# A one-core hybrid encoder layer: maxima and sums change tilings through DRAM, weights' factors queue behind turned weights' parts, the norm's weights come as one row, and the first gates' steps are reordered

## The chip, the cores and the metric

The kernel runs on one core of a Trainium2 chip. The core has five engines that run side by side, each with its own queue of instructions that it takes in order: TensorE (PE in the profile; its weight loads are PEld), VectorE (DVE), ScalarE (ACT), GpSimd (POOL) and SyncE (SP), which here issues nearly all DMAs. Data moves between DRAM and the on-chip memory by DMA; matmuls write into eight PSUM banks.

The metric is the device time of one execution in microseconds (us), as the median of several runs. The profile is one such execution with every instruction recorded.

## What is computed

One layer over 1024 positions of width 1024. The input is normalised and projected to nine parts; branch A is a gMLP with mixing inside chunks of 128 positions, branch B an attention of 8 heads over three dilated windows; both are gated, projected, summed, projected again, normalised and added to the input.

```python
h    = rms_norm(x, g_pre)
u_a, v_a, z_a, q_b, k_b, v_b, z_b, gate_a, gate_b = split(h @ w_in)
y_a  = spatial_gating(gelu(u_a), gelu(v_a), ln_g, ln_b, w_s, b_s) * silu(z_a)
y_b  = mixture_of_dilations(q, k, v) * silu(z_b)     # patterns (128,1), (512,4), (2048,16)
g_a, g_b = sigmoid(gate_a + b_gate[:1024]), sigmoid(gate_b + b_gate[1024:])
x    = x + rms_norm((g_a * (y_a @ w_pa) + g_b * (y_b @ w_pb)) @ w_o, g_post)
# mixture_of_dilations: one windowed softmax per pattern (scores minus ALiBi slope * distance),
# the outputs weighted by the softmax over the three log-denominators
```

## The kernel before

All products are made in float32 accuracy from parts: an operand is split into a high part (ScalarE copies it, L106 or L159) and a low part (VectorE or GpSimd subtracts, L108 or L160), and a product is three matmuls: high by high, high by low, low by high.

The program is written in an order, but it isn't the order in which the engines run it. A planner gives every engine its list ahead of time: at each moment of its own simulated clock it takes the instruction that is ready there, earlier written ones first. On the chip each engine then keeps to its list. Where the chip is slower than planned, an engine stands at the head of its list though later entries could run.

**Start (L202 to L342, pool `sp`).** The norm's weights `gpre` are loaded as 128 copies of one row (L218). 14 matmuls on an empty tile warm TensorE up (L223). `norm_tile` (L232) squares one tile of x on ScalarE (L240), makes the factor (L241, L164, L165), applies it and `gpre` on VectorE (L245), transposes the result on TensorE (L229) and splits it into `hT`. Around the first two tiles stand the loads and splits of the weights of the first product (`row_pair`, L315), and, one for each pair of rows, `spatial_weights` (L280): it turns four groups of the mixing weights (L290), splits them and stores them to `ws_d`, sums their rows (`wsR`, L297), and forms their bias (`wsB`, L302) for `wsb_d`. The values of branch B (`vb`) follow in five groups of products (L322); between their steps (`ahead`) the other tiles of x are normalised and summed. The last stores of `vb` (L258) go from tiles of the pool `sp`.

**Projections (L351 to L577, pool `ap`).** The other projections save one product in eight: `seven` (L373) makes seven half-size products from sums of the quarters of weights (`s1` to `s4`) and of the inputs (`r11`, `r21`, `r22`, `t1` to `t4`), in the order of `STEPS` (L348): p1, p6, p2, p7, p5, p4, p3. p2 goes on in p1's bank, p4 in p7's and p3 in p5's; so p1 must first be copied out of its bank (L388, tile `u2`). The first call is `gates(0)` (L483). Its working tiles lie where the pool `sp` was, so they wait until that pool's last users are done.

**Attention (L580 to L930).** A head's scores come in two tilings: `half` 1 has queries by residue and 512 keys, `half` 0 has chunks. For each of 8 blocks of a tiling VectorE subtracts the bias and takes the maximum (L667), and ScalarE makes the exponentials and their sum (L671); maximum and sum lie in `own`. `exchange` brings them into the other tiling: 16 small copies of 32 partitions for each half, on GpSimd for half 0 and on VectorE for half 1 (L684). `normalise` (L688) joins the two tilings' maxima and sums into one factor for each query and block (`nm`). `scale` (L705) applies it to the weights: `half` 1 on VectorE (L710), most of `half` 0 on ScalarE (L712), two blocks on GpSimd (L708). `weigh` (L718) then turns the weights on TensorE (`keys`, L730; the tiles are named `pb`, `pa` and `pe`), splits the turned weights into `pth` and `ptl` (L733), and multiplies them by the values (L749, L764). The turned weights alternate between two banks; a bank is free once `ptl` is made from it.

The main loop (L902) runs nine stages for each head: the stages of `weigh` for head h, the scores of head h+1 beside them, the queries and keys of head h+2, and as filler the steps of branch A's last product (`mlp_products`, L849; the tiles `pa`, L872 to L874, with its weights `wr_pa`, `wl_pa`). In stage 3 stand the value loads of the next head and `exchange` for half 0, in stages 6 and 7 `exchange` for half 1, in stage 8 `normalise` and the first factors, then the loads `va` and `ve` (L621, L622). Inside `weigh` the factors of stage i+2 follow the turned weights of stage i (L801).

Of the kernel before, what the change touches and what calls it, by code (L numbers as in the profile page):

```python
# [18 lines left out]
P = 128  # L19
# [17 lines left out]
def tile_hybrid_encoder(  # L37
# [120 lines left out]
    def split(hi, lo, src, low=nc.vector):  # L158
        nc.scalar.activation(hi, src, AF.Copy)  # L159
        low.tensor_tensor(lo, src, f32(hi), ALU.subtract)  # L160
# [29 lines left out]
    wo_d = hi_lo("wo", [2, KT, P, 512])  # L190
    wsb_d = dram.tile([4, P, 4, P], F32, name="wsb_d")
# [10 lines left out]
    with tc.tile_pool(name="start", bufs=1) as sp:  # L202
# [15 lines left out]
        nc.scalar.dma_start(gpre, g_pre.to_broadcast([P, D]))  # L218
# [3 lines left out]
        for _ in range(14):  # L222
            nc.tensor.matmul(pt, idle[:, :P], idle, start=True, stop=True)  # L223

        def transposed(hl, i, src, name):

            pt = bank("pv", name)
            for k in range(4):
                nc.tensor.transpose(pt[:, k * P:(k + 1) * P], src[:, k * P:(k + 1) * P], ident)  # L229
            split(*[t[:, :, i * P:(i + 1) * P] for t in hl], pt.rearrange("p (k n) -> p k n", k=4))  # L230

        def norm_tile(c, load=1):  # L232
# [6 lines left out]
            for j in range(2):  # L239
                nc.scalar.activation(sq, xt[:, 512 * j:512 * (j + 1)], AF.Square, accum_out=ss[:, j:j + 1])  # L240
            nc.vector.tensor_tensor(ss[:, 0:1], ss[:, 0:1], ss[:, 1:2], ALU.add)  # L241
            power(ss[:, 1:2], ss[:, 0:1], 1.0 / D)
            for j in range(2):
# [3 lines left out]
                transposed(hT[j][b], i, xs, f"xT{c}{j}")  # L247
# [59 lines left out]
        norm_tile(0, 0)  # L307
        rows = sp.tile([32, P], F32, name="rows")
        nc.scalar.dma_start(rows[0:16, :], b_gate.rearrange("o (k p) -> (o k) p", p=P))
        nc.scalar.dma_start(rows[16:32, :], ln_g.rearrange("o (k p) -> (o k) p", p=P))  # L310
# [40 lines left out]
    with tc.tile_pool(name="proj", bufs=1) as ap:  # L351
# [21 lines left out]
        def seven(name, units, product_of, use):  # L373
# [3 lines left out]
            acc, u2, u3 = {}, {}, {}  # L377
            for n, weights, rn in STEPS:
                into = {"p2": "p1", "p4": "p7", "p3": "p5"}.get(n)
                if into:  # L380
                    pss = acc[into]
                else:
                    pss = acc[n] = [bank(t, f"{name}{n}{u}") for u, t in enumerate(units[n].split())]
                product_of(n, weights, R[rn], pss, into is None)
                for u, ps in enumerate(pss):
# [12 lines left out]
                    if n in ("p5", "p4", "p3"):  # L398
                        use(*{"p5": (1, 1), "p4": (1, 0), "p3": (0, 1)}[n], u, c, c)
                yield  # L400

        def features(w, c0, name, use, pool=ap):
# [16 lines left out]
            return seven(name, {"p1": "mm", "p6": "tp", "p7": "sc", "p5": "sc"}, product_of, use)  # L419
# [63 lines left out]
        take(gates(0, pool=None))  # L483
# [96 lines left out]
    with tc.tile_pool(name="heads", bufs=1) as hp, tc.tile_pool(name="attn", bufs=1) as ap:  # L580
# [45 lines left out]
        def scores(h, res):  # L626
# [4 lines left out]
            own = res["own"] = hp.tile([P, 2, 8, 2], F32, tag="own", bufs=2, name=f"own{h}")  # L631
            wts = res["wts"] = {}
            order = [(1, (i, i + 1)) for i in (0, 2, 4, 6)] + [(0, (1, 2)), (0, (3, 4)), (0, (5, 6)), (0, (0, 7))]
            for half, pair in order:
# [31 lines left out]
                for t, idx in enumerate(pair):  # L666
                    nc.vector.tensor_tensor_reduce(st[:, t, :n], ps[:, t, :n], biases[t], -1.0, -NEG, ALU.add, ALU.min,  # L667
                                                   own[:, half, idx, 0:1])
                for t, idx in enumerate(pair):
                    wts[half, idx] = st[:, t, :n]  # L670
                    nc.scalar.activation(st[:, t, :n], st[:, t, :n], AF.Exp, bias=own[:, half, idx, 0:1], scale=-1.0,  # L671
                                         accum_out=own[:, half, idx, 1:2])
                yield

        def exchange(h, res, half):

            own = res["own"]
            if half == 0:
                res["oth"] = ap.tile([P, 2, 8, 2], F32, tag="oth", bufs=2, name=f"oth{h}")
            for i in range(4):  # L680
                for j in range(4):
                    src = own[32 * i:32 * (i + 1), 1 - half].rearrange("p (b a) s -> p b a s", a=4)[:, :, j, :]
                    dst = res["oth"][32 * j:32 * (j + 1), half].rearrange("p (b a) s -> p b a s", a=4)[:, :, i, :]
                    (nc.gpsimd, nc.vector)[half].tensor_copy(dst, src)  # L684
                if i % 2:
                    yield

        def normalise(h, res):  # L688
# [3 lines left out]
            dd = ap.tile([P, 2, 2, 8], F32, tag="dd", bufs=2, name=f"dd{h}")  # L692
            nm = ap.tile([P, 2, 8], F32, tag="nm", bufs=2, name=f"nm{h}")
            nc.vector.tensor_tensor(nm, own[:, :, :, 0], oth[:, :, :, 0], ALU.min)
            nc.vector.tensor_tensor(dd[:, 0], nm, own[:, :, :, 0], ALU.subtract)
            nc.vector.tensor_tensor(dd[:, 1], nm, oth[:, :, :, 0], ALU.subtract)
            nc.scalar.activation(dd, dd, AF.Exp)
            nc.vector.tensor_tensor(nm, dd[:, 0], own[:, :, :, 1], ALU.mult)
            nc.vector.tensor_tensor(dd[:, 1], dd[:, 1], oth[:, :, :, 1], ALU.mult)
# [4 lines left out]

        def scale(res, half, idx):  # L705
            w, f = res["wts"][half, idx], res["nm"][:, half, idx:idx + 1]
# [11 lines left out]
        def weigh(h, res):  # L718
# [6 lines left out]
            def keys(jobs, n, w, name):  # L725
# [7 lines left out]
                split(hi[:n, :w], lo[:n, :w], pt[:n, :w])  # L733
# [168 lines left out]
        for h in range(H):  # L902
# [4 lines left out]
            for i in range(9):  # L907
# [173 lines left out]
```

## Time and profile before

| | us |
|---|---|
| median of 3 runs | 1569.66 |
| lowest and highest run | 1565.85, 1571.71 |
| the profiled execution | 1570.04 |
| its span (first to last instruction) | 1568.3 |

Busy time by stretch of the span, in us:

| stretch | what runs | TensorE | VectorE | ScalarE | GpSimd |
|---|---|---|---|---|---|
| 0 to 134 | norm, values of B | 124.97 | 61.49 | 56.35 | 39.65 |
| 134 to 152 | first gates | 15.06 | 7.11 | 5.73 | 6.98 |
| 152 to 980 | projections, mixing | 823.52 | 500.07 | 342.12 | 460.02 |
| 980 to 1340 | heads, beside them branch A's last product | 327.82 | 241.97 | 234.40 | 188.02 |
| 1340 to 1568 | last products | 218.32 | 52.93 | 47.16 | 87.58 |

How to read the lines below. A line of the timeline has the start, the duration, the engine, the line of the kernel, the operation, output<-input, shapes and the count; in brackets stands the time that the engine sat idle before it and what it waited for last. SPq and ACTq are the queues that issue DMAs; a duration there is that of issuing, not of the transfer. A line of waits has who waited for whom, the total in us, how often, and the longest. The tables by stretch have the busy time and count of instructions for each engine, then the clock that TensorE was granted (1.00 is full speed), the busy share of the DMA engines, and GB/s.

### The profile page before, as it was taken

The page shows a single profiled execution, that of the slowest core. Times are in us where ns is not written, and L with a number is a line of the kernel's source. Part 1 is how long each engine was busy: PE and PEld are TensorE (multiplying, and loading weights), DVE is VectorE, ACT ScalarE, POOL GpSimd, SP SyncE. Part 2 cuts the span into 40 slices and gives each one's busy share as a digit, 9 for nine tenths or more (in the row PEclk, how much of TensorE's full clock was granted, in tenths as well). Part 3 has the DMA queues.
Part 4 walks back from the last instruction along what each step waited for, and adds up shares of the span by engine and source line. Part 5 has one row for each costly group of instructions (what it writes and reads, how often), then busy time and mean ns, then how long its engine had stood idle before and what let it go on. Part 6 is the DMA issues. An engine that isn't in the chain of part 4 may idle for free.

```text
span 1568.3 us, 22757 instructions
## 1 busy us (share of the span) xinstructions
PE 1509.7 (96%) x7863; PEld 1276.0 (81%) x7863; DVE 863.6 (55%) x1698; ACT 685.8 (44%) x1315; POOL 782.3 (50%) x711
## 2 busy tenths in 40 slices
PE   8999999999999999999999999989998889999998
PEld 4787999988888888788888888867887778878886
DVE  5722544476665675756665564577666767232112
ACT  5522433343433433343445454577666756331111
POOL 3412644465655555565555555446544554473132
PEclk9999999999999999999999999999998999999999
DMA  8455433344534452535434343497686766885531
GB/s 264 155 173 178 128 106 102 113 128 131 170 119 145 136 166 95 163 126 163 140 123 132 119 150 118 147 267 229 198 217 175 221 212 180 249 263 166 190 108 67
DMA packets 247940, 252.16 MB, mean 161 GB/s; under 512 B 14312, under 2 KB 187400, under 8 KB 247568
## 3 DMA queue, kind: packets, MB, share of 16 engines
q1 hardware_dynamic: 247456, 249.88, 51.0%
q8 instruction: 62, 1.02, 0.3%
q10 hardware_dynamic: 368, 0.82, 0.1%
q14 instruction: 54, 0.44, 0.1%
HBM read 174.10 MB, written 76.55 MB: 160 GB/s over the span
## 4 chain that ended last, share of the span: by engine, by line
PE 72%; DVE 8%; ACT 5%; issue 5%; DMA 4%; POOL 3%; SPq 1%; DVEq 0%; ACTq 0%; POOLq 0%
PE pb L996 2%; PE pb L995 2%; PE pb L997 2%; PE pa L872 2%; PE pa L873 2%; PE pa L874 2%; PE sg L527 2%; PE vb L154 1%; PE vb L156 1%; PE vb L155 1%; POOL out L1016 1%; ACT st L671 1%; DVE oth L684 1%; DMA vn<-v_d 1%; PE pr L749 1%
## 5 line engine op out<-in xcount | busy, mean ns | idle before, releaser
L108 POOL TENSOR_TENSOR wl_pa<-wr_pa,wh_pa 128x512 fp32r<-128x512 f32 x56 | 74.8, 1345 | 46.8 <-ACT wh_pa L106 44.2
L516 DVE TENSOR_SCALAR vn<-vn,mean,rstd 128x128 f32<-128x128 f32 x128 | 58.6, 512 | 35.2 <-DMA vn<-v_d 34.8
L671 ACT ACTIVATE st<-st,own 128x256 f32<-128x256 f32 (+1 forms) x128 | 62.7, 492 | 34.9 <-DVE own L667 34.6
L995 PE MATMUL pb<-yh,wh_pb 128*128 128x512 f32 x128 | 50.6, 395 | 1.7 <-ACT yh L159 1.7
L996 PE MATMUL pb<-yl,wh_pb 128*128 128x512 f32 x128 | 50.8, 396 | 0.5 <-DVE yl L160 0.3
L106 ACT ACTIVATE wh_pa<-wr_pa 128x512 fp32r<-128x512 f32 x64 | 38.7, 625 | 28.1 <-PE pa L873 13.2
L997 PE MATMUL pb<-yh,wl_pb 128*128 128x512 f32 x128 | 50.3, 393 | 0.0
L684 DVE COPY oth<-own 32x4 f32<-32x4 f32 x128 | 35.7, 279 | 14.1 <-ACT st L671 12.6
L1030 ACT ACTIVATE sq<-o 128x512 f32<-128x512 f32 x16 | 9.6, 598 | 74.7 <-PE o L1028 74.7
L730 PE MATMUL pb<-ident,st 128*128 128x128 f32 x128 | 21.6, 292 | 21.0 <-DVE ptla L160 15.6
L160 POOL TENSOR_TENSOR vl<-vn,vh 128x512 fp32r<-128x512 f32 x32 | 41.3, 1291 | 0.8 <-ACT vh L159 0.8
L999 POOL TENSOR_TENSOR mb<-thb,mb 128x512 f32<-128x512 f32 x16 | 20.6, 1286 | 41.7 <-DVE thb L998 32.2
L160 POOL TENSOR_TENSOR qcl<-q,qch 128x512 fp32r<-128x512 f32 x16 | 27.6, 1732 | 26.0 <-ACT qch L159 25.5
L817 POOL TENSOR_TENSOR o<-o,zt 128x512 f32<-128x512 f32 x16 | 20.6, 1292 | 36.3 <-DMA zt<-z_d 20.0
L1010 DVE TENSOR_TENSOR sso<-sso 128x1 f32<-128x1 f32 x8 | 1.3, 160 | 67.6 <-ACT sq L1030 67.6
L730 PEld LDWEIGHTS pb<-ident,st 128*128 128x128 f32 x128 | 16.2, 148 | 26.9 <-DVE ptla L160 17.7
L684 POOL COPY oth<-own 32x4 f32<-32x4 f32 x128 | 24.0, 187 | 23.8 <-ACT st L671 18.8
L667 DVE CUSTOM_DVE_ANT_0 st<-sc,tb 128x256 f32<-128x256 f32 x64 | 23.7, 420 | 21.0 <-PE sc L664 19.7
L165 POOL TENSOR_TENSOR sso<-sso,mhalf 128x1 f32<-128x1 f32 x8 | 4.4, 550 | 59.1 <-DVE sso L164 59.1
L160 DVE TENSOR_TENSOR ptlb<-pb,pthb 128x512 fp32r<-128x512 f32 x32 | 21.9, 687 | 20.5 <-ACT pthb L159 20.3
L108 POOL TENSOR_TENSOR wl_wos<-wr_wos,wh_wos 128x512 fp32r<-128x512 f32 x16 | 20.7, 1291 | 22.8 <-ACT wh_wos L106 22.8
L108 POOL TENSOR_TENSOR wl_vb<-wr_vb,wh_vb 128x512 fp32r<-128x512 f32 x14 | 18.8, 1352 | 23.8 <-ACT wh_vb L106 23.8
(2643 smaller groups left out, 5852.9 us busy)
## 6 DMA issues: line engine op xcount, KB each, us to landing
wr_pa<-in_w_proj_a_dram SPq DMA_DIRECT2D x32, 512.0 KB, 5.5
wr_g<-in_w_in_dram SPq DMA_DIRECT2D x16, 512.0 KB, 3.5
wr_va<-in_w_in_dram SPq DMA_DIRECT2D x16, 512.0 KB, 3.8
wr_u<-in_w_in_dram SPq DMA_DIRECT2D x16, 512.0 KB, 4.1
wr_z<-in_w_in_dram SPq DMA_DIRECT2D x16, 512.0 KB, 3.7
vn<-v_d SPq DMA_DIRECT2D x32, 256.0 KB, 2.7
y_d<-s SPq DMA_DIRECT2D x32, 256.0 KB, 3.1
wr_yf<-y_d SPq DMA_DIRECT2D x16, 512.0 KB, 6.2
```

Source lines behind the costliest of these rows:

```text
L106: nc.scalar.activation(hi, src, AF.Copy)
L108: low.tensor_tensor(lo, src, f32(hi), ALU.subtract)
L160: low.tensor_tensor(lo, src, f32(hi), ALU.subtract)
L516: nc.vector.tensor_scalar(vn[:, c, :], vn[:, c, :], mean[:, 4 * b + c, 0:1], rstd[:, 4 * b + c:4 * b + c + 1], op0=ALU.subtract, op1=ALU.mult)
L527: nc.tensor.matmul(pg[:, 256 * c:256 * (c + 1)], w[:, 2 * cp + c, :], wst, start=(w is vh and c == 0), stop=(w is vl and c == 1), skip_gro ...
L671: nc.scalar.activation(st[:, t, :n], st[:, t, :n], AF.Exp, bias=own[:, half, idx, 0:1], scale=-1.0, accum_out=own[:, half, idx, 1:2])
L684: (nc.gpsimd, nc.vector)[half].tensor_copy(dst, src)
L730: nc.tensor.transpose(pt[:n, c0:c0 + P], src, ident)
L872: nc.tensor.matmul(pss[m], lh[:, k, :], rh, start=(q == 0 and k == 0), stop=False)
L995: nc.tensor.matmul(ps, lh, rh, start=(k == 0), stop=False)
L996: nc.tensor.matmul(ps, lh, rl, start=False, stop=False)
L997: nc.tensor.matmul(ps, ll, rh, start=False, stop=(k == KT - 1))
```

## The change

1. **Norm's weights as one row.** `g_pre` is loaded into one partition; two matmuls with a row of ones spread it over 128 partitions, and ScalarE copies the result. The warm-up is 4 matmuls before and 8 behind these. A one-column square is put first on ScalarE.
2. **Order at the start.** The splits of the first weights on ScalarE are queued behind the first tile's squares; the loads of `b_gate` and `ln_g` too. The four `spatial_weights` move from between the weight loads into the steps of the first product, behind the first tile's transposes on TensorE and its squares on ScalarE.
3. **First gates.** `gates(0)` runs p1, p6, p5, p2, p7, p4, p3; the use of p5 waits in its bank until p7 has been used.
4. **Maxima and sums through DRAM.** `exchange` stores `own` of one tiling to DRAM and loads it back with four loads of 32 partitions, all on SP; the layouts of `own`, `oth`, `dd` and `nm` change with it.
5. **Factors behind parts.** `scale` is queued behind the last turned weights' split on ScalarE and VectorE, save for the first two blocks of a head and the first head's.

```diff
+    own_d = [[dram.tile([P, 16], F32, name=f"own_d{i}{j}") for j in range(2)] for i in range(2)]
...
-        nc.scalar.dma_start(gpre, g_pre.to_broadcast([P, D]))
+        grow = gpre[0:1, :]
+        nc.scalar.dma_start(grow, g_pre)
+        first = wpool.tile([P, 512], F32, tag="th", bufs=2, name="first")
+        ones = first[0:1, :P]
+        nc.vector.memset(ones, 1.0)
+        nc.scalar.activation(first[:, P:P + 1], mhalf, AF.Square)
...
-        for _ in range(14):
-            nc.tensor.matmul(pt, idle[:, :P], idle, start=True, stop=True)
+        warm(4)
+        for j, pg in enumerate(banks("mm mm", "gpre")):
+            nc.tensor.matmul(pg, ones, grow[:, 512 * j:512 * (j + 1)], start=True, stop=True)
+            nc.scalar.activation(gpre[:, 512 * j:512 * (j + 1)], pg, AF.Copy)
+        warm(8)
...
-            wv += row_pair(w_in, OFF_VB, k, "vb0", (nc.gpsimd, nc.vector) if k < 4 else (nc.gpsimd, nc.gpsimd))
+            with tc.issue_after(squared.ins):
+                wv += row_pair(w_in, OFF_VB, k, "vb0", (nc.gpsimd, nc.vector) if k < 4 else (nc.gpsimd, nc.gpsimd))
...
-            spatial_weights(k // 2)
+        with tc.issue_after(squared.ins):
+            nc.scalar.dma_start(rows[0:16, :], b_gate.rearrange("o (k p) -> (o k) p", p=P))
+            nc.scalar.dma_start(rows[16:32, :], ln_g.rearrange("o (k p) -> (o k) p", p=P))
+        def spatial(q):
+            def emit():
+                with tc.issue_after(turned.ins), tc.issue_after(squared.ins):
+                    spatial_weights(q)
+            return emit
...
-        for cb, cs, tags, ahead in ((0, (0, 4), "mm mm", {2: norm(1), 5: norm(5)}),
+        for cb, cs, tags, ahead in ((0, (0, 4), "mm mm", {1: spatial(0), 2: norm(1), 3: spatial(1), 4: spatial(2), 5: norm(5),
+                                                          6: spatial(3)}),
...
+                if n == "p5" and not u3:
+                    kept.append((n, pss))
+                else:
+                    results(n, pss)
+                    while n == "p7" and kept:
+                        results(*kept.pop())
...
-        take(gates(0, pool=None))
+        take(gates(0, pool=None, steps=[STEPS[i] for i in (0, 1, 4, 2, 3, 5, 6)]))
...
-            own = res["own"] = hp.tile([P, 2, 8, 2], F32, tag="own", bufs=2, name=f"own{h}")
+            own = res["own"] = hp.tile([P, 2, 4, 2, 2], F32, tag="own", bufs=2, name=f"own{h}")
...
-            for i in range(4):
-                for j in range(4):
-                    src = own[32 * i:32 * (i + 1), 1 - half].rearrange("p (b a) s -> p b a s", a=4)[:, :, j, :]
-                    dst = res["oth"][32 * j:32 * (j + 1), half].rearrange("p (b a) s -> p b a s", a=4)[:, :, i, :]
-                    (nc.gpsimd, nc.vector)[half].tensor_copy(dst, src)
-                if i % 2:
-                    yield
+            d = own_d[h % 2][half]
+            nc.sync.dma_start(d, res["own"][:, 1 - half].rearrange("p a b s -> p (a b s)"))
+            yield
+            for j in range(4):
+                src = d[:, 4 * j:4 * (j + 1)].rearrange("(a i) s -> i a s", a=4)
+                nc.sync.dma_start(res["oth"][32 * j:32 * (j + 1), half].rearrange("p a b s -> p a (b s)"), src)
+            yield
...
+        parts = []
         def scale(res, half, idx):
-            w, f = res["wts"][half, idx], res["nm"][:, half, idx:idx + 1]
+            with ExitStack() as after:
+                for i in parts:
+                    after.enter_context(tc.issue_after(i.ins))
+                scale_tile(res, half, idx)
+        def scale_tile(res, half, idx):
+            w, f = res["wts"][half, idx], res["nm"][:, half, idx % 4, idx // 4:idx // 4 + 1]
...
-                split(hi[:n, :w], lo[:n, :w], pt[:n, :w])
+                parts[:] = split(hi[:n, :w], lo[:n, :w], pt[:n, :w])
...
-                    for tile_ in TILES[0] + TILES[1]:
+                    for tile_ in TILES[0]:
+                        scale_tile(heads[h + 1], *tile_)
+                    for tile_ in TILES[1]:
                         scale(heads[h + 1], *tile_)
```

`tc.issue_after(i)` fixes only an order: what is written inside comes behind `i` in the list of `i`'s engine. It adds no wait for `i` to finish.

More of the change, by code (lines that the diff above doesn't have):

```diff
@@ L221, in tile_hybrid_encoder, with warm @@
         pt = bank("tp", "warm")
-        for _ in range(14):
-            nc.tensor.matmul(pt, idle[:, :P], idle, start=True, stop=True)
+        def warm(n):
+            for _ in range(n):
+                nc.tensor.matmul(pt, idle[:, :P], idle, start=True, stop=True)
+        warm(4)
[3 more added lines that the diff above has]
+        warm(8)
         def transposed(hl, i, src, name):
@@ L228, in transposed @@
             for k in range(4):
-                nc.tensor.transpose(pt[:, k * P:(k + 1) * P], src[:, k * P:(k + 1) * P], ident)
+                last = nc.tensor.transpose(pt[:, k * P:(k + 1) * P], src[:, k * P:(k + 1) * P], ident)
             split(*[t[:, :, i * P:(i + 1) * P] for t in hl], pt.rearrange("p (k n) -> p k n", k=4))
+            return last
         def norm_tile(c, load=1):
@@ L246, in norm_tile @@
                                                op1=ALU.mult)
-                transposed(hT[j][b], i, xs, f"xT{c}{j}")
+                last = transposed(hT[j][b], i, xs, f"xT{c}{j}")
+            return squared, last
         def v_out(c, cb, ps):
@@ L305, in spatial_weights @@
             nc.sync.dma_start(wsb_d[q].rearrange("p g n -> p (g n)"), wb)
-        norm_tile(0, 0)
+        squared, turned = norm_tile(0, 0)
         rows = sp.tile([32, P], F32, name="rows")
-        nc.scalar.dma_start(rows[0:16, :], b_gate.rearrange("o (k p) -> (o k) p", p=P))
-        nc.scalar.dma_start(rows[16:32, :], ln_g.rearrange("o (k p) -> (o k) p", p=P))
         wv = []
@@ L371, in weight_operands, with seven, results @@
             return lambda n: sum_of(n) if isinstance(n, str) else quart(n)
[L373 to L384, printed above, removed]
+        def seven(name, units, product_of, use, steps=STEPS):
+            acc, u2, u3, kept = {}, {}, {}, []
+            def results(n, pss):
                 for u, ps in enumerate(pss):
@@ L399, in seven, with features @@
                         use(*{"p5": (1, 1), "p4": (1, 0), "p3": (0, 1)}[n], u, c, c)
+            for n, weights, rn in steps:
+                into = {"p2": "p1", "p4": "p7", "p3": "p5"}.get(n)
+                if into:
+                    pss = acc[into]
+                else:
+                    pss = acc[n] = [bank(t, f"{name}{n}{u}") for u, t in enumerate(units[n].split())]
+                product_of(n, weights, R[rn], pss, into is None)
+                if n == "p5" and not u3:
+                    kept.append((n, pss))
+                else:
+                    results(n, pss)
+                    while n == "p7" and kept:
+                        results(*kept.pop())
                 yield
-        def features(w, c0, name, use, pool=ap):
+        def features(w, c0, name, use, pool=ap, steps=STEPS):
             raw = [raw_tile(w[4 * j * P:4 * (j + 1) * P, c0:c0 + 256].rearrange("(k p) n -> p k n", p=P),
@@ L417, in product_of @@
                                      skip_group_check=True)
-            return seven(name, {"p1": "mm", "p6": "tp", "p7": "sc", "p5": "sc"}, product_of, use)
+            return seven(name, {"p1": "mm", "p6": "tp", "p7": "sc", "p5": "sc"}, product_of, use, steps)
         def tokens(w, c0, name, use):
```

28 lines of the change are left out of this document (13 added, 15 removed).

## The prediction

> **What bounds the kernel now.** I read the page first, then the busy time by stretches of the span, then what TensorE (PE) waited for, then the timeline around each wait.
>
> ```profile
> span 1568.3 us, 22757 instructions
> PE 1509.7 (96%) x7863; PEld 1276.0 (81%) x7863; DVE 863.6 (55%) x1698; ACT 685.8 (44%) x1315; POOL 782.3 (50%) x711
> ...
> core 0: us, PE busy (x) PEld busy (x) DVE busy (x) ACT busy (x) POOL busy (x), PEclk, DMA share, GB/s
> 0.00:16.00 16.00, 10.81 (x29) 4.32 (x29) 5.24 (x15) 6.59 (x14) 2.50 (x8) 0.83 0.83 282
> 134.00:152.00 18.00, 15.06 (x60) 11.96 (x59) 7.11 (x10) 5.73 (x10) 6.98 (x5) 0.91 0.83 291
> 152.00:980.00 828.00, 823.52 (x4363) 711.29 (x4362) 500.07 (x816) 342.12 (x554) 460.02 (x345) 1.00 0.42 133
> 980.00:1340.00 360.00, 327.82 (x1891) 280.56 (x1890) 241.97 (x682) 234.40 (x548) 188.02 (x251) 0.96 0.71 206
> ```
>
> TensorE is busy 96% of the span, so only its holes can be won. The long middle, 152 to 980 us, has 4.5 us of holes in 828 and is not edited. The edits lie in the other three stretches: the start; the seam where the first gates begin (134 to 152), with 2.9 us idle and the clock at 0.91; and the attention heads, 980 to 1340, with 360 - 327.8 = 32.2 us idle and a mean clock of 0.96. The waits of TensorE name those holes (total, times, longest):
>
> ```profile
> PE pb L730 <- DVE ptla L160: 15.6, 5, 7.5
> PE pb L730 <- DVE st L710: 5.5, 1, 5.5
> PE pa L730 <- DVE ptle L160: 3.0, 1, 3.0
> PE g0p L412 <- ACT g0u L388: 2.9, 1, 2.9
> PE pe L730 <- DVE ptla L160: 2.0, 1, 2.0
> ```
>
> Four of the five are transposes of attention weights (L730) that wait for VectorE (DVE), 26.1 us together.
>
> **Start: one row of g_pre, squares first, spatial weights later.**
>
> ```profile
> q1 hardware_dynamic: 195, 0.63, 37.2%
> q10 hardware_dynamic: 148, 0.52, 24.9%
> ...
> 8.22 0.63 ACT L106 ACTIVATE wh_vb<-wr_vb 128x512 fp32r<-128x512 f32 x1 [3.71 <-DMA wr_vb<-in_w_in_dram]
> 8.76 0.58 ACT L240 ACTIVATE sqx<-xt 128x512 f32<-128x512 f32 x1
> ...
> 10.57 1.09 PE L290 MATMUL wsT<-ident,wsr 128*128 128x128 f32 x4 [3.23 <-DMA wsr<-in_w_spatial_dram]
> ...
> 12.35 1.86 PE L297 MATMUL wsR<-wf,col 128*1 128x512 f32 x2 [0.69 <-ACT wf L291]
> ...
> 15.95 0.79 PE L154 MATMUL vb<-wh_vb,hT00h 128*128 128x512 f32 x1
> ```
>
> The first two rows are the DMA queues of the first 6 us: ScalarE's (q10) moved 0.52 MB, the g_pre broadcast, beside 0.63 MB of the queue that brings the first x tile (q1). The squares of that tile began at 8.76, behind a weight split (L106) that had itself waited for its weights; the first product came 7.2 us later, at 15.95. With one row in place of the broadcast, the tile is through when 0.52 of those 1.15 MB have moved: 2.7 us at an even rate, later since no bytes move at first, 6 at most. I take 4, and the squares from 4.3. Out of the 7.2 us fall the second weight split between the squares (0.6) and wsR (1.86); two copies of the replicated row go in on ScalarE (0.6 each, I count one on the path): 7.2 - 2.5 + 0.6 = 5.3, first product at 9.6, 6.3 us earlier. TensorE gets 2.95 us of wsT and wsR back inside the product, leaving 3.4. The two matmuls that replicate the row (about 1 us each, wsR being two halves) stand in the wait for x, where warm-up matmuls stood; the small square only brings the table load forward. Moved loads: b_gate and ln_g are read only at L335, behind the third group of products, and wsr, shift, rowsum and the ws_d and wsb_d stores have no reader but the spatial steps and a stage far later; later issue costs nothing there, and the SP queue passes them with x and weights. I take **-3.5**. Bounds: -7, if none of the 2.95 returns (it falls into product holes), and +2, if the product then waits for its weights and for wsr, as the 3.23 us row shows it did.
>
> **Gates: p5 moved ahead of p2.**
>
> ```profile
> 139.28 0.39 PE L414 MATMUL g0p<-t2l,wh_g0p 128*128 128x512 f32 x1
> 139.51 0.39 PE L416 MATMUL g0p<-t2h,wl_g0p 128*128 128x512 f32 x1
> 142.18 0.60 ACT L388 ACTIVATE g0u<-g0p 128x512 f32<-128x512 f32 x1 [7.09 <-DMA vb_l<-vhl]
> 142.83 0.50 PE L412 MATMUL g0p<-hT10h,wh_g0p 128*128 128x512 f32 x1 [2.94 <-ACT g0u L388]
> 143.63 0.59 PE L412 MATMUL g0p<-hT10h,wh_g0p 128*128 128x512 f32 x1
> 147.01 0.43 PE L416 MATMUL g0p<-hT10h,wl_g0p 128*128 128x512 f32 x1
> ```
>
> p2 adds into p1's bank, so ScalarE must first copy p1 to a tile (L388) whose memory is free only when the last v store has landed. p5 needs neither: its weight sum s1 is made for p6 anyway, and its split finds ScalarE idle for 7.09 us. Its 12 matmuls at 0.227 us (from p6's rhythm, 139.28 to 139.51) fill 2.7 of the 2.94 us. The 8 matmuls from 143.63 to 147.01 took 3.38 us where 1.82 are due: another 1.6 us of slow clock after the hole. Sum **-4.3**, bounds 0 (p5's split is late) to -5. p7's split, formerly covered by p2, still has p2's 2.7 us; p5's result waits on u3 in its own bank, with no reader hurried.
>
> [...]
>
> **Attention: the exchange through DRAM, and weights' factors behind parts.** First the path at one head change (head 1), then the longest hole (head 4):
>
> ```profile
> 1087.59 2.95 DVE L684 COPY oth<-own 32x4 f32<-32x4 f32 x8 [0.47 <-ACT st L671]
> ...
> 1089.86 7.97 SPq L113 DMA_DIRECT2D wr_pa<-in_w_proj_a_dram  x2
> ...
> 1092.41 3.88 DVE L710 TENSOR_SCALAR st<-st,nm 128x256 f32<-128x256 f32 x8
> 1096.21 1.01 DVE L160 TENSOR_TENSOR ptla<-pa,ptha 128x512 fp32r<-128x512 f32 x2
> ...
> 1097.28 0.66 PE L730 MATMUL pb<-ident,st 128*128 128x128 f32 x4 [2.26 <-DVE ptla L160]
> ...
> 1193.93 3.83 DVE L684 COPY oth<-own 32x4 f32<-32x4 f32 x8
> ...
> 1201.40 6.16 DVE L710 TENSOR_SCALAR st<-st,nm 128x256 f32<-128x256 f32 x6
> 1207.48 0.68 DVE L160 TENSOR_TENSOR ptla<-pa,ptha 128x512 fp32r<-128x512 f32 x1
> ...
> 1209.75 1.11 PE L730 MATMUL pb<-ident,st 128*128 128x128 f32 x4 [7.51 <-DVE ptla L160]
> ...
> 1210.00:1216.00 6.00, 6.00 (x27) 5.67 (x27) 1.12 (x3) 0.60 (x1) 0.00 (x0) 0.55 0.51 146
> ```
>
> Last exponential; copies to the other tiling; normalise (1090.54 to 1092.41, 1.87 us); eight factors; only then the old head's parts ptla, whose bank the new head's transposes need. The second edit queues six of the eight factors behind the parts: in head 1 it takes 3.88 x 6/8 + 1.01 = 3.9 us out of the path. The first replaces the copies, whose groups are
>
> ```profile
> L684 DVE COPY oth<-own 32x4 f32<-32x4 f32 x128 | 35.7, 279 | 14.1 <-ACT st L671 12.6
> L684 POOL COPY oth<-own 32x4 f32<-32x4 f32 x128 | 24.0, 187 | 23.8 <-ACT st L671 18.8
> ...
> 1097.92 1.93 SPq L622 DMA_DIRECT2D ve<-vb_h  x4
> ...
> ve<-vb_h SPq DMA_DIRECT2D x32, 16.0 KB, 2.9
> ...
> q<-q_d SPq DMA_DIRECT2D x16, 256.0 KB, 4.3
> ```
>
> so 35.7 us leave VectorE and 24.0 us POOL, off the path but for the last copies. In come 16 stores and 64 loads on SP, with pieces of 64 and 16 bytes, that no row shows. The nearest is ve, 16 KB: four issues in 1.93 us, 2.9 to landing. Store, then the last of four loads: 2.9 + 3 x 0.48 + 2.9 = **7.2 us** (with the 4.3 of a 256 KB load, 10.0; from below, the 2.95 of the copies). In SP's order the loads wait for the store, so everything queued behind (q, k, bias, w_proj_a, y loads, ma_d and o_d stores) waits some 2.9 us too, 16 times; w_proj_a has three buffers and seven split pairs ahead of TensorE, which cover that.
>
> Head 1: 1087.59 + 7.2 + 1.87 + 0.97 (two factors) = 1097.6, against 1097.28: +0.3. So it goes in the four shorter ptla holes (15.6 - 7.5 = 8.1 us together): **+1**. Head 4: 1193.93 + 7.2 + 1.87 + 0.97 = 1204.0, against 1209.75: -5.8, and the hole shrinks to under 2, so the 0.55 clock of the 6 us after it (2.7 us) comes back: **-8.5**. Head 0 has no old parts; there the longer exchange lies bare on the 5.5 us hole: 7.2 - 2.95, **+4**. The holes of 3.0 and 2.0 us in head 6 have copies and normalise ahead of the parts on VectorE; I take back half, 2.5, and clock in head 4's proportion (2.7 x 5.0 / 7.5 = 1.8): **-4.3**. Attention: +1 - 8.5 + 4 - 4.3 = **-7.8**, bounds -29 and +19 (rivals 3 and 2). The changed layouts of own, oth, dd and nm keep the element counts: 0, at most 0.05 us on each of nine operations a head.
>
> [...]
>
> **Sum.** -3.5 - 4.3 - 7.8 = -15.6 on the profiled execution's 1570.0 (span 1568.3 and 1.7 around it); the median of the runs, 1569.7, lies 0.4 lower, within their scatter. Forecast **1554.4 us**.
>
> **Rivals.**
> 1. The exchange eats what the factors free. For it: DMA is busy 71% in this stretch, and q takes 4.3 us. At 10.0 us heads 0 to 5 are each 2.8 later, +16.8: 1571. Against: VectorE and POOL are 60 us lighter.
> 2. Slower than before: the loads stand behind a blocked transfer on SP. At 1089.86 SP sat 7.97 us on w_proj_a, just where head 1's loads would go; released at 1097.83, they put the transposes at 1097.83 + 1.4 + 2.9 + 1.9 + 1.0 = 1105, 7.5 late, plus some 1.6 of clock: 9 a head. Three heads: +27, 1581. It decides from two such heads on (15.6 / 9). Against: the order is planned from readiness, and POOL, which frees those buffers, is relieved.
> 3. The holes all go but head 0's: 26.1 - 5.5 = 20.6 idle plus 8 of the 14 us of clock (0.04 x 360) and 7.8 at the start and gates: 1533.6. For it: lighter VectorE; against: the longer path.
> 4. The start moves but its product then waits for weights: 1558.
> 5. The order holds, but the parts are late for another reason (ScalarE's ptha), so head 4 keeps its hole: 1563.
>
> **How the numbers follow.** Forecast 0.46 (itself 1546 to 1564), rival 1 0.20, 2 0.12, 3 0.08, 4 0.08, 5 0.06. A measurement of this kernel tells about 0.5% (7.8 us) from no change, so faster means below 1562: forecast, 3 and 4, 0.62; the same: 1 and 5, 0.26; slower: 2, 0.12. The range, 1535 to 1580, leaves out most of rival 2 and half of 3.
>
> **What would show it.** The first vb product near 9.6 us; the gates' hole near 140 us under 0.5 and no slow matmuls behind it; ptla before the factors at each head; head 4's hole under 2 us; head 0's over 9. Wrong if the loads of oth show long issue waits on SP, or normalise begins over 9 us after the last exponential.

## The result, and the profile after

The changed kernel is **slower**: 1592.9 us (median of 4 runs, 1591.2 to 1597.0) against 1570.2 for the kernel before beside it, a ratio of 1.0145 [1.0127, 1.0163], some 22.8 us. The forecast was 1554.4 us, its range ended at 1580: the sign was wrong. The profiled execution took 1592.6 us. One run of the start alone and one of the exchange on GpSimd's queue, both below, were some 100 us longer at a lower clock (1682.8 us at 0.84, 1736.7 at 0.83); medians and ratios leave them out.

First the page of the kernel after, then its busy time by stretches, with the columns as before: three of the prediction's, and last the one from 980 us to the first product of the last projection, which is the same work as 980 to 1380.96 us in the kernel before.

```profile
span 1590.8 us, 22645 instructions
PE 1529.3 (96%) x7865; PEld 1286.3 (81%) x7865; DVE 833.1 (52%) x1571; ACT 683.8 (43%) x1318; POOL 755.5 (47%) x583
```

```profile
134.00:152.00 18.00, 17.90 (x79) 14.49 (x78) 5.81 (x8) 5.95 (x10) 2.84 (x3) 1.00 0.66 245
152.00:980.00 828.00, 822.56 (x4353) 709.83 (x4353) 503.29 (x818) 340.87 (x553) 462.40 (x347) 1.00 0.42 134
980.00:1340.00 360.00, 325.76 (x1785) 272.76 (x1783) 200.95 (x523) 218.98 (x512) 150.88 (x113) 0.95 0.66 194
980.00:1403.08 423.08, 388.26 (x2110) 325.26 (x2109) 221.96 (x568) 248.68 (x576) 184.56 (x140) 0.95 0.66 195
```

```profile
980.00:1380.96 400.96, 368.78 (x2097) 314.96 (x2095) 251.65 (x696) 250.60 (x576) 210.94 (x268) 0.97 0.72 209
```

The last row is the kernel before's. VectorE lost 30 us of work and GpSimd 26 in the heads, as planned, and the same stretch of matmuls took 22 us more. TensorE's idle time in it grew by 2.6 us only (34.8 for 32.2). The rest is the lower clock (0.95 for 0.97, some 7 us before rounding) and gaps too short to count as idle: lags of 0.1 to 1.5 us between the starts of neighbouring matmuls over their usual spacing, at full clock, number some 90 to 100 and sum to some 22 us, where they were some 40 and 10 us (estimates from all their starts in the two traces; the count hangs a little on what is taken as usual). Landmarks of the two traces place the loss:

| us | before | after | later by |
|---|---|---|---|
| first gates matmul | 134.3 | 139.8 | 5.5 |
| first product of `va0` with `hT10h`, behind the gates | 169.7 | 171.9 | 2.2 |
| first maxima of head 0 | 1033.5 | 1036.2 | 2.7 |
| normalise of head 0 begins | 1051.2 | 1068.4 | 17.3 |
| last product with values (`pc`) | 1358.4 | 1380.5 | 22.1 |
| last instruction | 1568.3 | 1590.8 | 22.5 |

So in these two traces the start lost 5.5 us, the gates won 3.3, and the heads lost about 19. Now what TensorE, and SP at the loads of `oth`, waited for after (total, times, longest), and the timeline of the places that the prediction spoke of:

```profile
PE pb L773 <- DVE st L753: 13.9, 7, 5.2
PE xT L242 <- DVE xt L259: 5.8, 3, 4.4
PE pa L915 <- ACT ya0310h L159: 5.4, 1, 5.4
...
SPq L719 <- DMA own_d<-own: 11.5, 8, 4.2
```

```profile
4.06 3.78 PE L234 MATMUL gpre<-gpre,first 1*128 1x512 f32 x4
10.55 0.60 ACT L254 ACTIVATE sqx<-xt 128x512 f32<-128x512 f32 x1 [2.08 <-PE warm L230]
13.07 2.93 POOL L108 TENSOR_TENSOR wl_vb<-wr_vb,wh_vb 128x512 fp32r<-128x512 f32 x2
13.13 3.42 DVE L259 SCALAR_TENSOR_TENSOR xt<-xt,ss,gpre 128x512 f32<-128x512 f32 x2 [0.67 <-POOL ss L164]
17.37 0.78 PE L154 MATMUL vb<-wh_vb,hT00h 128*128 128x512 f32 x1
...
148.26 0.50 PE L445 MATMUL g0p<-hT10h,wh_g0p 128*128 128x512 f32 x1
...
1052.45 0.44 SPq L656 DMA_DIRECT2D ve<-vb_l  x1
1053.00 0.89 SPq L113 DMA_DIRECT2D wr_yf<-y_d  x2
...
1054.49 1.31 SPq L714 DMA_DIRECT2D own_d<-own  x2
...
1061.35 3.64 SPq L719 DMA_DIRECT2D oth<-own_d  x8
1068.44 0.17 DVE L728 TENSOR_TENSOR nm<-own,oth 128x16 f32<-128x16 f32 x1
...
1140.79 0.43 SPq L633 DMA_DIRECT2D ta<-in_alibi_a_dram  x1
1150.98 1.79 SPq L655 DMA_DIRECT2D va<-vb_h  x4
...
1156.76 0.84 SPq L850 DMA_DIRECT2D zt<-z_d  x2
1160.78 2.54 POOL L860 TENSOR_TENSOR o<-o,zt 128x512 f32<-128x512 f32 x2 [14.86 <-DMA zt<-z_d]
```

What to see. The transposes no longer wait for `ptla`; they wait for the factors (`st`). In head 0 both stores stand on SP behind loads of values, `y` and branch A's weights and are issued at 1054.49. The loads, eight and not four, follow 5.5 us after the second store was issued, when both have landed, so normalise begins 14 us behind the first store where 7.2 was reckoned. In head 2 SP stands still for 9.8 us (1141.22 to 1150.98) at the loads of `va`, and GpSimd stands 14.9 us at `o`, whose `zt` is queued behind them.

### The profile page after: what moved, and what is told of

Read it like the earlier page. It is cut to its first block, busy times and chain, and to the rows that moved or that the text cites. A ratio compares the mean times of both kernels' runs of the same rounds, so it can differ in the third digit from the quotient of the medians.

```text
span 1590.8 us, 22645 instructions
## 1 busy us (share of the span) xinstructions
PE 1529.3 (96%) x7865; PEld 1286.3 (81%) x7865; DVE 833.1 (52%) x1571; ACT 683.8 (43%) x1318; POOL 755.5 (47%) x583
## 4 chain that ended last, share of the span: by engine, by line
PE 71%; DVE 7%; ACT 6%; DMA 6%; issue 6%; POOL 3%; SPq 1%; ACTq 0%; DVEq 0%; POOLq 0%
PE pa L916 2%; PE pa L915 2%; PE pa L917 2%; PE pb L1040 2%; PE pb L1041 2%; ACT st L705 2%; PE pb L1042 2%; PE vb L154 2%; PE vb L156 2%; PE vb L155 2%; PE sg L561 2%; DMA wr_pa<-in_w_proj_a_dram 1%; POOL out L1061 1%; PE pr L792 1%; DMA vn<-v_d 1%
## 5 line engine op out<-in xcount | busy, mean ns | idle before, releaser
L108 POOL TENSOR_TENSOR wl_pa<-wr_pa,wh_pa 128x512 fp32r<-128x512 f32 x56 | 71.3, 1287 | 97.0 <-ACT wh_pa L106 84.8
L106 ACT ACTIVATE wh_pa<-wr_pa 128x512 fp32r<-128x512 f32 x64 | 38.5, 626 | 17.3 <-DMA wr_pa<-in_w_proj_a_dram 16.8
L159 POOL TENSOR_TENSOR qcl<-q,qch 128x512 fp32r<-128x512 f32 x16 | 29.3, 1832 | 31.9 <-ACT qch L159 30.9
L773 PE MATMUL pb<-ident,st 128*128 128x128 f32 x128 | 24.4, 301 | 14.3 <-DVE st L753 13.9
L159 ACT ACTIVATE pthb<-pb 128x512 fp32r<-128x512 f32 x32 | 18.8, 591 | 37.9 <-PE pb L773 37.8
L159 DVE TENSOR_TENSOR qrl<-q,qrh 128x512 fp32r<-128x512 f32 x16 | 22.6, 1411 | 19.0 <-ACT qrh L159 19.0
L108 POOL TENSOR_TENSOR wl_wos<-wr_wos,wh_wos 128x512 fp32r<-128x512 f32 x16 | 20.7, 1291 | 22.8 <-ACT wh_wos L106 22.8
L159 DVE TENSOR_TENSOR ptla<-pa,ptha 128x512 fp32r<-128x512 f32 (+1 forms) x32 | 19.5, 621 | 21.9 <-ACT ptha L159 21.9
```

The lines of the kernel that those rows point to most:

```text
L159: return nc.scalar.activation(hi, src, AF.Copy), low.tensor_tensor(lo, src, f32(hi), ALU.subtract)
L773: nc.tensor.transpose(pt[:n, c0:c0 + P], src, ident)
```

## The experiments

**The four edits one by one.** Each is the kernel before with one group of the diff: the start (1 and 2 of the list), the gates (3), the factors (5), the exchange (4).

> The start edits alone (one row of g_pre, order, spatial weights later); exchange, factors and gates as before. Theory 'the start costs': the squares wait for the warm-up behind the replicating matmuls, first squares near 10.5 us, first vb product near 17.4, first gates matmul near 139.8 (134.3 before): about 1575.5 us. Rival 'the start only looks late, its loss is returned in the later groups': within 1.5 us of before, 1570.

> The reordered first gates alone. Both theories: the 2.94 us hole at 140 us closes, the first product with hT10h comes 3 to 4.3 us earlier and stays so to the end: 1566 to 1567 us. If the planner's later lists shift with it, the gain may be lost in the heads: 1570.

> The factors behind the parts alone, with the copies between partitions as before. Theory 'the exchange through DRAM costs all of the +20 us of the heads, the factors gain': the holes at the transposes shrink from 26 to some 12 us, 1556 to 1562 us. Rival 'the order of the factors is itself what costs, by delaying the weights of later stages': slower than before, 1575 to 1590.

> The exchange through DRAM alone, factors ordered as before. Theory 'the exchange costs': head 0's first transposes are some 13 us later, the other heads lose about 2 each: 1590 to 1605 us. Rival 'the factors' order costs': only head 0's 4 us and little else, 1572 to 1578.

| edit alone | median, us | ratio to before |
|---|---|---|
| start | 1574.0 | 1.0021 [1.0005, 1.0038] |
| gates | 1567.9 | 0.9984 [0.9967, 1.0001] |
| factors | 1564.6 | 0.9961 [0.9949, 0.9973] |
| exchange | 1590.0 | 1.0115 [1.0081, 1.0148] |

The exchange is the loss, and the factors gain; what gates and start do is at the edge of their intervals. But the four ratios multiply to 1.008, and the whole change gave 1.0145: some 10 us more, give or take some 7 by the five intervals together. So factors and exchange were put together:

> The exchange through DRAM and the factors behind parts, start and gates as before. If the two worked on different holes, 0.4% less than the exchange alone: 1584 us. Theory 'with the exchange the parts come ahead of the factors anyway, so the second edit has nothing left to win': as the exchange alone or a little over, 1588 to 1594.

It measured 1.0125 [1.0108, 1.0143], no better than the exchange alone: the gain of the factors is gone. The waits of TensorE at `pb` tell why; first for the factors alone, then the exchange alone, then both:

```profile
PE pb L738 <- DVE ptla L159: 2.5, 1, 2.5
```

```profile
PE pb L731 <- DVE st L711: 11.9, 4, 5.3
```

```profile
PE pb L739 <- DVE st L719: 12.3, 5, 5.1
```

Before, `pb` waited 15.6 us for parts. The factors' order takes 13 of these away. The exchange takes them all away too, since the factors then come so late that the parts are done first; what is left are waits for the factors, which their order can't help. That is 6 of the 10 us; the other 4 lie within the error.

**Where the exchange costs.** The layouts with copies (nothing through DRAM), one half through DRAM, and all heads but head 0. `through_dram` stands for False, `half == 0`, `half == 1` and `h > 0`; behind it come the store and the loads of the change:

```diff
+            if through_dram:
...
+                return
+            for i in range(4):
+                for j in range(4):
+                    (nc.gpsimd, nc.vector)[half].tensor_copy(res["oth"][32 * j:32 * (j + 1), half, i],
+                                                             res["own"][32 * i:32 * (i + 1), 1 - half, j])
```

> The new layouts of own, oth, dd and nm, with copies between partitions (one copy of four neighbouring numbers a partition where before there were two pieces) and nothing through DRAM. All theories of the exchange: as before, 1568 to 1572 us. Rival 'the layouts cost, by strided operands in normalise and the reductions': 1580 or more.

> Only half 0 (GpSimd's copies, begun in stage 3) goes through DRAM; half 1 stays with VectorE's copies. Theory 'the latency of the late half costs': little is lost except at head 0, where both halves come last: 1570 to 1576 us. Rival 'GpSimd, freed of its copies, works on splits beside normalise and slows VectorE's small operations': most of the 20 us stays, 1582 to 1590.

> Only half 1 (VectorE's copies, behind the last exponential) goes through DRAM; half 0 stays with GpSimd's copies. Theory 'the latency of the late half costs': nearly the whole loss of the exchange alone, 1584 to 1590 us. Rival 'freed GpSimd is the cause': 1572 to 1578.

> Head 0 keeps its copies, heads 1 to 7 go through DRAM. Theory 'head 0's bare chain (normalise 14 us later) carries most of the loss': 1574 to 1580 us. Rival 'the loss lies in heads 1 to 7, in the many short waits of TensorE on parts, and head 0 is covered by branch A's products': 1584 to 1590.

Layouts 1.0003 [0.9990, 1.0017]: they cost nothing. Half 1 alone 1.0093 [1.0077, 1.0108]. Half 0 alone 1.0147 [1.0130, 1.0163]: the half that has slack costs more than the late one, and no less than both together (1.0115 [1.0081, 1.0148]), so latency on the way to normalise can't be the whole story. All heads but the first 1.0062 [1.0040, 1.0084]: head 0 carries about half of the 18 us, the other seven the other half. Neither theory had that shape: the latency of the late half forecast half 1 rightly and missed half 0 by 18 us, and a freed GpSimd came out 4 us low on half 0 and 8 on half 1.

**The DMAs without the exchange.** The copies stay and feed normalise; beside them the same stores and loads run on SP, into a tile that nobody reads. The loads are written right behind their store, where the exchange has a step of other work between. Two more kernels take pieces of that away: loads that read what the head before stored, so that no load waits for a landing (56, since head 0 has nothing to read), and the 16 stores alone.

```diff
+            if half == 0:
+                res["junk"] = ap.tile([P, 2, 4, 2, 2], F32, tag="junk", bufs=2, name=f"junk{h}")
+            d = own_d[h % 2][half]
+            nc.sync.dma_start(d, res["own"][:, 1 - half].rearrange("p a b s -> p (a b s)"))
+            for j in range(4):
+                src = d[:, 4 * j:4 * (j + 1)].rearrange("(a i) s -> i a s", a=4)
+                nc.sync.dma_start(res["junk"][32 * j:32 * (j + 1), half].rearrange("p a b s -> p a (b s)"), src)
             for i in range(4):
                 for j in range(4):
                     (nc.gpsimd, nc.vector)[half].tensor_copy(
...
```

> Copies between partitions as before (layouts new), and beside them the same 16 stores and 64 loads on SP as in the exchange through DRAM, into tiles that nobody reads. Theory 'SP's order costs: stores that wait for the exponentials and loads that wait for the store hold up the loads behind them': half or more of the 18 to 20 us of the exchange alone, 1580 to 1590 us. Rival 'the latency of the exchange on the way to normalise costs': at most 3 us over before, 1570 to 1573.

> As copies_and_idle_dmas, but each head's 8 idle loads read what the head before stored and stand ahead of the stores, so that no load waits for a store to land; the stores still wait for the exponentials. Theory 'loads behind the landing block SP': most of the 39 us goes, 1572 to 1585 us. Rival 'the stores' wait or the count of issues and small pieces': 1595 to 1612.

> As copies_and_idle_dmas, but only the 16 stores, no loads. Theory 'loads behind the landing': 1570 to 1576 us. Rival 'stores that wait on SP for the exponentials hold up the loads behind them': 1585 or more.

| beside the copies, on SP | ratio to before | us |
|---|---|---|
| 16 stores | 1.0109 [1.0088, 1.0129] | +17 |
| 16 stores, 56 loads that don't wait for a landing | 1.0167 [1.0144, 1.0190] | +26 |
| 16 stores, 64 loads behind their landing | 1.0247 [1.0230, 1.0265] | +39 |

This is the decisive series: transfers that nothing depends on cost as much as the exchange and more. A wait of normalise can't be it, and 8 KB out and 8 KB back for each half are few bytes (from 980 to 1400 us the DMA engines' busy share is 0.63 with all of them, 0.73 before); what is left is what they do to SP's list: their waits there, their own issuing (0.3 to 0.45 us each at the median), and the order that is planned around them. The stores wait there for the exponentials, the loads for the stores, and each step of the series adds some 9 to 17 us. Of the theories in the last two expectations, that the stores' wait (or the count of issues) costs comes nearer; the wait for the landing adds 13 us. What SP stood for them, in all, first with the stores alone, then with all idle DMAs:

```profile
SPq L683 <- ACT st L672: 19.0, 9, 4.2
```

```profile
SPq L683 <- ACT st L672: 23.7, 7, 6.4
SPq L686 <- DMA own_d<-own: 13.3, 8, 3.9
```

The timeline of the kernel with all idle DMAs, near head 2:

```profile
1138.92 0.42 SPq L596 DMA_DIRECT2D krl<-k_d  x1
1145.79 1.77 SPq L622 DMA_DIRECT2D va<-vb_h  x4
...
1151.59 0.43 SPq L600 DMA_DIRECT2D tb<-in_alibi_b_dram  x1
1152.13 0.84 SPq L813 DMA_DIRECT2D zt<-z_d  x2
1154.56 0.42 DVE L668 CUSTOM_DVE_ANT_0 st<-sc,tb 128x256 f32<-128x256 f32 x1 [5.39 <-DMA tb<-in_alibi_b_dram]
1156.29 2.65 POOL L823 TENSOR_TENSOR o<-o,zt 128x512 f32<-128x512 f32 x2 [14.71 <-DMA zt<-z_d]
```

What GpSimd waited for `zt` in all, in the kernel before and then in this one, each with its busy time by stretch; last the same wait in the exchange alone:

```profile
POOL o L817 <- DMA zt<-z_d: 20.0, 3, 9.7
980.00:1400.00 420.00, 385.56 (x2160) 327.78 (x2159) 259.43 (x704) 257.68 (x589) 226.50 (x279) 0.96 0.73 214
```

```profile
POOL o L823 <- DMA zt<-z_d: 63.3, 7, 14.7
980.00:1400.00 420.00, 371.57 (x1996) 312.59 (x1995) 252.66 (x686) 237.73 (x559) 191.10 (x256) 0.91 0.63 184
```

```profile
POOL o L818 <- DMA zt<-z_d: 18.8, 2, 12.6
```

SP stands 6.5 us at `va`, whose buffers the head's last products hold; behind it come the biases (`ta`, `te`, `tb`) and `zt`. VectorE stands at its first maximum for 5.4 us without its bias, GpSimd at `o` for 14.7 without `zt`, and with it GpSimd's splits for branch A that come later in its list. It is the picture of head 2 in the changed kernel. TensorE pays by 14 us more of idle time in 420 and by a clock of 0.91 for 0.96. In the kernel before, the same jam (`zt` issued behind the values, GpSimd waiting over 9 us) comes only in two of the eight heads. But this one jam doesn't account for the smaller losses: the exchange alone waits 18.8 us in all for `zt` and the stores alone 22.6, about as much as before, and they lose 18 and 17 us.

What stays open: the planner makes every engine's list anew for each of these kernels, so part of the cost may lie in a worse order and part in waiting within it, and the series doesn't part the two. The traces show that the order did move. From the first maxima to the last projection, against the copies with the new layouts (which keep the order of the kernel before), some 12% of TensorE's products stand in another order with the stores alone, 21% with the loads that don't wait, 27% with all idle DMAs and 29% in the exchange alone, and of SP's other transfers 11%, 26%, 27% and 27%. The factors' edit moved 1% of TensorE's. The halves' losses don't add either: 0.93% and 1.47% apart, 1.15% together.

The same exchange issued from GpSimd's queue:

```diff
-            nc.sync.dma_start(d, res["own"][:, 1 - half].rearrange("p a b s -> p (a b s)"))
+            nc.gpsimd.dma_start(d, res["own"][:, 1 - half].rearrange("p a b s -> p (a b s)"))
...
-                nc.sync.dma_start(res["oth"][32 * j:32 * (j + 1), half].rearrange("p a b s -> p a (b s)"), src)
+                nc.gpsimd.dma_start(res["oth"][32 * j:32 * (j + 1), half].rearrange("p a b s -> p a (b s)"), src)
```

> The exchange through DRAM, alone of the change, but issued from GpSimd's queue instead of SP's. Theory 'SP's order costs' (head 0's loads of oth issued at 1058.7 though its maxima were ready near 1049): head 0's normalise begins near 1058 instead of 1065, 1572 to 1580 us. Rival 'latency': within 4 us of the exchange on SP, 1586 to 1594.

It took 1631.3 us, 1.0385 [1.0361, 1.0408]: worse than on SP, so neither expectation held. The theory of SP's order, which forecast 1572 to 1580 here, isn't confirmed by it, nor refuted if GpSimd's list suffers in SP's place. Only its time is used here; that GpSimd then stands at these stores and loads itself, with its splits behind, is argued and not shown.

**The start.** First without the move of the spatial weights; then with the first pair's low parts on VectorE instead of GpSimd; then with the warm-up in a bank of its own.

```diff
+            spatial_weights(k // 2)
...
-{1: spatial(0), 2: norm(1), 3: spatial(1), 4: spatial(2), 5: norm(5),
-6: spatial(3)}
+{2: norm(1), 5: norm(5)}
...
-(nc.gpsimd, nc.vector) if k < 4 else
+(nc.vector, nc.vector) if k < 2 else (nc.gpsimd, nc.vector) if k < 4 else
...
-        pt = bank("tp", "warm")
+        pt = bank("sc", "warm")
```

> The start edits without the move of the spatial weights (these stay between the weight loads; one row, warm-up and squares first as in the change). Theory 'the move costs, by putting 2.95 us of turned and replicated spatial weights a quarter into the product': 3 us less than all start edits together, 1570 to 1572 us. Rival 'the row costs, its two products of 3.8 us and the warm-up stand ahead of the squares': as all start edits, 1574 to 1576.

> The start edits alone, with the first two weights' low parts on VectorE instead of one of them on GpSimd. Theory 'GpSimd beside VectorE slows the first scaling (1.7 us a half instead of 0.7)': the two scalings take 1.4 us instead of 3.4, the first transposes come some 1 to 2 us earlier after the squares, 1571.5 to 1574 us. Rival: as the start edits alone, 1574 to 1576.

> The start edits alone, with the warm-up in a bank that the first squares don't use. Theory 'the warm-up's bank costs': first squares 2 to 3 us earlier than 10.5 us, first product near 14.5, first gates matmul near 135 to 137, 1570 to 1573 us. Rival 'what the squares win is lost again, since the spatial weights in the product set the pace': as the start edits alone, 1574 to 1576.

| start edits alone, and | median, us | ratio to before |
|---|---|---|
| spatial weights kept | 1573.1 | 1.0005 [0.9990, 1.0021] |
| first splits on VectorE | 1577.6 | 1.0043 [1.0029, 1.0057] |
| warm-up in another bank | 1569.6 | 0.9983 [0.9973, 0.9992] |

By the times the bank is the cause: with the warm-up in another bank, 0.2% slower becomes 0.2% faster, and the two intervals lie apart. The first square is written to the one bank of the tag `tp`, and the warm-up holds that bank until it ends, behind the two products that spread the row (3.78 us, recorded as four matmuls). In another bank the squares come at 4.88 us. From the timeline of that kernel, then of the one with splits on VectorE:

```profile
4.88 0.60 ACT L254 ACTIVATE sqx<-xt 128x512 f32<-128x512 f32 x1 [2.10 <-DMA xt<-in_x_dram]
...
10.68 0.48 DVE L300 MEMSET shift<- 2x512 f32 x1 [2.19 <-PE warm L230]
11.63 1.39 DVE L259 SCALAR_TENSOR_TENSOR xt<-xt,ss,gpre 128x512 f32<-128x512 f32 x2
...
12.42 1.32 PE L242 MATMUL xT<-ident,xt 128*128 128x128 f32 x8 [1.91 <-DVE xt L259]
13.76 0.73 PE L154 MATMUL vb<-wh_vb,hT00h 128*128 128x512 f32 x1
```

```profile
13.14 1.41 DVE L259 SCALAR_TENSOR_TENSOR xt<-xt,ss,gpre 128x512 f32<-128x512 f32 x2 [0.67 <-DMA xt<-in_x_dram]
14.28 1.41 POOL L108 TENSOR_TENSOR wl_vb<-wr_vb,wh_vb 128x512 fp32r<-128x512 f32 x1 [1.17 <-ACT wh_vb L106]
14.47 2.36 DVE L108 TENSOR_TENSOR wl_vb<-wr_vb,wh_vb 128x512 fp32r<-128x512 f32 x2
```

How late the shared bank makes the squares differs between executions. In the profile of the start alone, which has the changed kernel's start, the two products took 2.23 us and the rest of the warm-up 1.47 (3.78 and 2.74 after). The squares came at 7.72 and the first product at 14.55, ahead of 15.95 before, where 10.5 and 17.4 were expected; and still the first gates matmul came at 137.0 (134.3 before). So the first product's time in one trace doesn't tell what a start is worth.

The mechanism expected of the splits on VectorE was right and its gain was not: without GpSimd's splits beside them the two scalings take 1.41 us instead of 3.42, but the splits then stand on VectorE ahead of `hT00l`, and the kernel is slower by 0.43%. Keeping the spatial weights in place may win some 2 us; the intervals overlap.

**What is left without the exchange.** The gates and the factors; then these with the start whose warm-up has its own bank (every edit but the fourth):

> Gates reordered and factors behind parts, start and exchange as before. If the two gains add (0.16% and 0.39% apart): 0.45 to 0.65% faster, 1560 to 1563 us. If the factors' order only helps at one clock phase: within 0.2% of before.

> Start (warm-up in its own bank), gates and factors; the exchange by copies as before. If the parts add up: 0.5 to 0.8% faster than before, 1558 to 1563 us. If the start still costs its 0.2%: 1562 to 1564.

They took 1559.3 us, 0.9930 [0.9914, 0.9946], and 1558.3 us, 0.9916 [0.9900, 0.9931]: **both beat both kernels**, the second by some 13 us. The second's row for the heads, and its waits at the turned weights:

```profile
980.00:1340.00 360.00, 337.10 (x1943) 285.48 (x1942) 251.29 (x681) 234.94 (x555) 187.96 (x252) 0.97 0.72 213
```

```profile
PE pb L772 <- DVE st L752: 5.7, 2, 5.2
...
PE pb L772 <- DVE ptla L159: 2.6, 1, 2.6
```

TensorE is busy 337 us of 360 in the heads, against 328 before and 326 in the changed kernel. With copies the waits for `ptla` at `pb` shrink from 15.6 us to 2.6, and only head 0's hole of 5.2, which has no old parts, stands as before.

## Why the prediction was wrong, step by step

- **The exchange's place on SP: the step that failed.** The prediction saw that in SP's order everything behind the loads waits for the store, and costed it at nothing, because the weights of branch A have three buffers. The runs put 39 us on just these DMAs beside the copies, 17 on the stores alone, and 18 on the exchange. What is queued there is not only those weights: biases and `zt` have no such cover, and VectorE and GpSimd stood in order behind them, 5.4 and 14.7 us in one head of the kernel with all idle DMAs. Nor did the prediction count that the planner would make the lists anew around these DMAs; how the cost parts between waiting and order stays open. Rival 2 (slower, 1581) was the right kind, loads behind a blocked transfer on SP, with the wrong culprit: SP stands at stores that wait for exponentials, at loads behind their landing and at `va`, not at w_proj_a. It had 0.12 and ended 12 us too low.
- **The path of 7.2 us.** In heads 1 to 7 near it: from the store that follows the last exponential to the start of normalise 6.7 to 9.8 us, 8.2 at the mean. In head 0 wrong: both halves go together at the end, the first store is issued 1.5 us after the last exponential, behind value and weight loads, the loads can start only 5.5 us after the second store, and there are eight of them at 0.45 us. Normalise came 14.6 us later against the work around it (17.3 less the 2.7 of the landmark before it), +4 was reckoned. Its nine operations were left at 1.87 us; in heads 1 to 4, where they took 1.7 before, they took 3.5 to 4.6. (Before, they took 3.6 to 9.0 in heads 0, 5 and 6 too, so 1.87 was the best case.) Rows of the exchange alone, head 1, show what changed:

```profile
1093.77 2.50 POOL L108 TENSOR_TENSOR wl_pa<-wr_pa,wh_pa 128x512 fp32r<-128x512 f32 x2
1093.88 1.22 DVE L696 TENSOR_TENSOR dd<-nm,own 128x16 f32<-128x16 f32 x1
...
1096.83 0.16 DVE L699 TENSOR_TENSOR nm<-dd,own 128x16 f32<-128x16 f32 x1
```

  An operation on tiles of this shape takes 0.16 us alone and 1.2 beside GpSimd's split, which now falls there.
- **Factors behind parts.** Right where the copies stay (six of 1570 us alone, and head 4's hole went from 7.5 to 2.5 us, as forecast under or near 2), void in company of the exchange. The prediction reckoned both edits together, head by head, and in form it came so: the transposes wait for the factors. By its sums the holes at `pb` come to some 20 us (9.5 in head 0, 1.7 in head 4, 9.1 in four others); 13.9 were measured. So the loss of the heads is not in the holes that the sum went by.
- **Head 0's hole over 9 us.** Not seen: the planner put branch A's products there, and TensorE waited 5.4 us for their input (`ya0310h`) instead.
- **Gates.** Right: the hole is gone (17.90 of 18 us busy, clock 1.00), 3.3 us won between the two traces against 4.3 forecast, 2.2 by the medians of the edit alone, whose interval just reaches no change. From the first gates matmul to the first product of `va0` with `hT10h` the four kernels with the new order take 31.9 to 32.1 us, the others 33.3 to 36.5.
- **Start.** The reckoning of the data was right and its place was not. Squares from 4.3 us were forecast; with the bank free they come at 4.88. The step missed is the bank that the warm-up shares with the squares: 10.55. With it the start costs 0.2%, without it wins 0.2% (some 2.7 us, forecast 3.5). The two products that spread the row were counted as 2 us; they took 3.78 in four profiles and 2.2 to 2.4 in two. With the bank free the first product comes at 13.8, not 9.6: VectorE stands until 10.68 at a memset of `shift` that waits for the warm-up, and the scalings stand behind it. No run leaves the warm-up out, so what it does for TensorE isn't shown.
- **The signs named for a wrong forecast** both came: SP waited 11.5 us at the loads of `oth`, and normalise began 15.4 us behind head 0's last exponential (1.5 before).

Without the exchange the terms of start and gates, -3.5 and -4.3, and the 6 us that the factors won alone come to 14 us; 13 were measured, with the start's bank changed. The forecast fell by the one term that put new transfers with waits into a queue that many share.

## What to carry to other kernels

Here small DMAs that wait on a shared queue cost 17 to 39 us with nobody reading them. Before a small copy is replaced by a store and a load on a shared queue, list the loads behind it and who stands in order for them, and try the DMAs without a reader first: that shows what they cost apart from their own latency (here more than the exchange itself). Where a planner orders the lists, look also at how much of the order a few new entries move. Two edits that close the same hole needn't add; price each with the other in place. When a start is re-ordered, look at the PSUM banks too: here a warm-up that shared a bank with the first squares held them until 10.55 us, and in a bank of its own they came at 4.88.

## What the hardware showed that was not expected

- Some of VectorE's operations on two operands of the on-chip memory lengthened beside GpSimd's subtractions: 128x512 scalings from 0.71 to 1.71 us each (1.41 against 3.42 for two), 128x16 ones from 0.16 to 1.2 and more (1.45 at most, in the trace before). The splits `ptla`, which read one operand from PSUM, stayed at 0.69 on 128x512, also beside GpSimd's subtractions (at 1349.75 us in the trace before). The small copies of the kernel before, 0.16 us alone, took up to 1.5 beside GpSimd's operations on 128x512 tiles; they read one operand. What makes the one kind lengthen and the other not, no run here shows.
- The first gates matmul came anywhere from 133.8 to 137.3 us in thirteen profiled executions whose start was the same code, and at 137.0 and 139.8 in the two with the changed start, so a single profile can't judge a start edit of 3 us: the +5.5 us in the table of landmarks is 3.3 by the ratio of the start alone.
